# Splitting the output weights of a hybrid attention layer one piece at a time instead of back to back

## The chip, the cores and the metric

The kernel is one program on one core of a Trainium2 chip. The number that counts is the device time of one execution in microseconds; lower is better. Engines: PE (TensorE, matmuls; PEld its weight loads), DVE (VectorE), ACT (ScalarE), POOL (GpSimd), SP (SyncE, which here only issues DMAs). Each engine works through its own list of instructions strictly in order and waits at an instruction until what it needs is there.

## The reference, cut to what matters

Two layers (DEPTH = 2). Each normalises 1280 tokens (256 prompt, 1024 sample), projects them once, runs two mixers on the result, and maps both outputs by one matrix `w_out` back to the model width of 1024. The mixers are multi-head latent attention with 8 heads and a gated DeltaNet with 4 heads.

```python
o_a = mla_attention(q_nope, q_pe, kv[..., :NOPE], kpe_all, kv[..., NOPE:]) * jax.nn.silu(g_a)
...
o_b = rmsnorm(o_b, o_norm).reshape(B, S, D_B) * jax.nn.silu(g_b)
out = jnp.einsum('bse,ed->bsd', jnp.concatenate([o_a, o_b], axis=-1), w_out)
x = x + gate * out
```

Large products are made of three reduced-precision matmuls each: an operand is split into a high part (the value rounded to the fp32r format) and a low part (the value minus the high part), and high·high, high·low and low·high are added. `w_out` (1024 x 1024) is one of the operands that are split, once per layer.

## The kernel before

**Stages of a layer.** Input projection (tiles `zp`, weights `wh`/`wl`), DeltaNet scans, then attention head by head, then the output stage (`wop`). Attention runs beside the end of the DeltaNet work. It is done in the transposed form: keys on the partitions, 512 queries in each of two halves along the free axis.

**One attention head, `main(h)`.** For the sample tokens it walks 10 key tiles of 128 keys (kt = 2 to 11). Per key tile PE makes the scores of each half in three matmuls (`sp`), ACT makes their exponentials (`pe<-sp`, 128x512 each), and PE multiplies the exponentials of the tile before with the values (`po`). The sum of the exponentials over the keys is kept apart: the tiles `pe` are added into an accumulator (`pe<-pe,pe`, 128x1024) on POOL, except at key tiles 7 and 11 and for the very last tile, where DVE adds (`VADD`, `VLAST`). So a head has six adds on POOL and three on DVE, and the last three links of this chain are a POOL add, a DVE add and the final DVE add. `finish(h)` then sums the accumulator over the partitions with a matmul (`pd`), takes the reciprocal on DVE, multiplies by the gate on POOL and by the output on DVE (`ob`), and writes the result to DRAM. A shorter block for the 256 prompt tokens (128x256 tiles) stands at the start of each head.

**Beside it, `prep(h+1)`.** The keys and queries of the next head are projected (`kp`, `qp`), and for each query the largest score is found (`pm` matmuls, DVE reduces `at<-pm`). These maxima are transposed (`mxt`), written to DRAM (`mx_d<-at`) and read back as one row (`at<-mx_d`), which the next head's scores need.

**The output weights, `pre_c`.** A thread of its own that starts when the last DeltaNet head is done. It loads `w_out` in 16 pieces of 128x512 into a ring of 8 buffers `wor`, and splits each piece with `split_wo`: ACT casts the high part (`woh<-wor`) and POOL subtracts for the low part (`wol<-wor,woh`). A load of piece 9 or later waits until the piece that had its buffer has been split. After the last piece `pre_c` starts the threads of the output stage.

**What sets the order.** All work is written as Python generators ("threads"). `Sched.run` (line 105) keeps a clock per engine with estimated costs and hands out the instruction that can start earliest, ties by a priority table `PR`; `pre_c` has the lowest priority among the attention threads (`prec` = 5). A thread can `yield` the name of a flag and is not continued before some thread has set it. `main` sets a flag `m{h}.{kt-2}` at each key tile of head h (line 1582); `prep` uses these flags to pace itself. The result is one fixed list per engine. When the estimate leaves PE idle for long, the scheduler puts in small filler matmuls (`spare`).

**Names.** Tile names carry running numbers that differ between the two programs; `pe_8841` and `wol_9012` are numbers of layer 0, `pe_19174` of layer 1. All instructions come from one helper, so in the profile they all stand on line L312.

Of the kernel before, what the change touches and what calls it, by code (L numbers as in the profile page):

```python
# [16 lines left out]
P = 128  # L17
# [7 lines left out]
NK = T + PAST  # L25
DEPTH = 2
HA = 8
# [367 lines left out]
def body(tc, I, O):  # L395
# [8 lines left out]
    def open_pool(stack, name, bufs=1, **k):  # L404
        return Pool(stack.enter_context(tc.tile_pool(name=name, bufs=bufs, **k)), bufs)
# [153 lines left out]
    def mixer(l, hhl):  # L559
        sd = Sched()  # L560
# [831 lines left out]
        def open_rest():  # L1392
            nonlocal bp
            ws.close()
            bp = open_pool(bs, f"b{l}", bufs=1, side="right")
            t5 = hp.tile([P, 4096], F32R, tag="hh2", name="at5")
            t6 = hp.tile([P, 4096], F32R, tag="hl2", name="at6")
            f6 = t6[:, NK:].bitcast(F32)
            at["ga"] = [f6[:, 0:640], f6[:, 640:1280]]
            at["ob"] = [bp.tile([P, 512], F32, tag=f"ob{i}", name=f"ob{i}") for i in range(2)]  # L1400
            wv = at["wv"] = bp.tile([P, 512], F32, tag="wv", name="wv")
            SY.dma_start(wv, I["w_v"][l])
            Kt.append((t5[:, 0:NK], t6[:, 0:NK]))
            Q.append((t5[:, NK : NK + T], t5[:, NK + T : NK + 2 * T]))
            for h in range(HA):
                if h:
                    sd.add(PR['prep'], prep(h))
                if h % 2 == 0:
                    sd.add(PR['vv'], vproj(h // 2))
                sd.add(PR['main'], main(h))  # L1410
            sd.add(PR['prec'], pre_c())
# [228 lines left out]
        def pre_c():  # L1640
            yield f"done{HB-1}"
            gs.close()
            cw = open_pool(cs, f"cw{l}", bufs=1)
            xs_ = ExitStack()
            cx = open_pool(xs_, f"cx{l}", bufs=1)
            yield 0
            for e in range(8):
                hi = cw.tile([P, DM], F32R, tag=f"woh{e}", name=f"woh{e}")
                lo = cw.tile([P, DM], F32R, tag=f"wol{e}", name=f"wol{e}")
                wo.append((hi, lo))  # L1650
                for hf in range(2):
                    raw = cx.tile([P, 512], F32, tag="wor", name="wor", bufs=8)
                    sl = slice(hf * 512, hf * 512 + 512)
                    SY.dma_start(raw, I["w_out"][l, e * P : (e + 1) * P, sl])
                    wor.append((hi[:, sl], lo[:, sl], raw))
                    yield 0
                    if len(wor) >= 8:
                        split_wo(wor.pop(0), e)
            while wor:
                split_wo(wor.pop(0), len(wor) // 2)  # L1660
                yield 0
            xs_.close()
            c0 = open_pool(cs, f"c0{l}", bufs=1)
            cc_[0] = c0
            load_gate(0, c0)
            for t in range(2):
                sq[t] = c0.tile([P, 2], F32, tag=f"sq{t}", name="sq")
            sd.add(PR['ldc'], load_c())
            sd.add(PR['mm'], mm_thread())

        wor = []

        def split_wo(w, e):
            hi, lo, raw = w
            S.copy(hi, raw)
            (V if len(wor) % 2 < VWO else G).tensor_tensor(lo, raw, hi.bitcast(F32), op=ALU.subtract)
# [14 lines left out]
        def load_c():  # L1691
            for t in range(NT):
                if t == 1:
                    yield f"main{HA-2}"
                    yield f"vv{HA//2-1}"
                    yield f"prep{HA-1}"
                    m1 = hp.tile([P, 4, DM], F32, tag="hh1", name="m1")
                    n1 = hp.tile([P, 2, 8, P], F32R, tag="hl1", name="n1")
                    x, of, cc_["tm"] = m1[:, 0], m1[:, 1].rearrange("p (a b) -> p a b", a=8), m1[:, 2]
                elif t == 2:  # L1700
                    yield "tm0"
                    yield "C"
                if t >= 3:
                    yield f"fin{t-3}"
                if t != 1:
                    x = cc_[0 if t % 3 == 0 else 1].tile([P, DM], F32, tag="x", name="x", bufs=1 if t % 3 == 0 else 2)
                SY.dma_start(x, (I["x"] if l == 0 else xs)[t * P : (t + 1) * P, :])
                if t == 0:
                    yield "attn0"
                pool = cc_.get(t % 2)  # L1710
                if t != 1:
                    of = pool.tile([P, 8, P], F32, tag="of", name="of")
                SY.dma_start(of, o_d[:, :, t * P : (t + 1) * P].rearrange("e p t -> p e t"))
                if t >= 2:
                    yield f"mm{t-2}"
                if t == 1:
                    oh, ol = n1[:, 0], n1[:, 1]
                else:
                    oh = pool.tile([P, 8, P], F32R, tag="oh", name="oh")
                    ol = pool.tile([P, 8, P], F32R, tag="ol", name="ol")  # L1720
                V.tensor_copy(oh, of)
                G.tensor_tensor(ol, of, oh.bitcast(F32), op=ALU.subtract)
                yield 0
                xt[t], ot[t] = x, (oh, ol)
                sd.flag(f"ld{t}")

        def load_gate(t, pool):
            gb[t] = pool.tile([P, DM], F32, tag="gbc", name="gbc", bufs=1)
            SY.dma_start(gb[t], gate_d[l, t // 2 : t // 2 + 1, :].to_broadcast([P, DM]))
# [25 lines left out]
        def mm_thread():  # L1755
            for t in range(NT):
                yield f"ld{t}"
                oh, ol = ot[t]
                x = xt[t]
                if t < 2:  # L1760
                    s2[t], jk = sq[t], cc_[0].tile([P, 512], mybir.dt.bfloat16, tag="jk", name="jk")
                else:
                    s2[t], jk = [cc_[1].tile([P, n], d, tag=f"s{n}", name=f"s{n}", bufs=3 if n == 2 else 1) for n, d in ((2, F32), (512, mybir.dt.bfloat16))]
                for hf in range(2):
                    pt = yield from bank("wop")
                    cs = slice(hf * 512, hf * 512 + 512)
                    for e in range(8):
                        for i, (a, w) in enumerate(((oh, wo[e][0]), (oh, wo[e][1]), (ol, wo[e][0]))):
                            PE.matmul(pt, a[:, e, :], w[:, cs], start=(e == 0 and i == 0), stop=(e == 7 and i == 2))
                        yield 0  # L1770
                    if t == 1:
                        tm = cc_["tm"][:, cs]
                    elif t:
                        tm = cc_[1].tile([P, 512], F32, tag="tm", name="tm", bufs=2)
                    else:
                        tm = cc_[0].tile([P, 512], F32, tag="of", name="tm0")
                    with sd.side(1):
                        V.tensor_tensor(tm, pt, gb[0 if t < 2 else 2][:, cs], op=ALU.mult)
                        free(pt)
                        V.tensor_tensor(x[:, cs], x[:, cs], tm, op=ALU.add)  # L1780
                        S.activation(jk, x[:, cs], AF.Square, accum_out=s2[t][:, hf : hf + 1])
                        if hf:
                            sd.add(PR['fc'], fin(t))
                    if not t and hf:
                        sd.flag("tm0")
                sd.flag(f"mm{t}")
# [43 lines left out]
    for l in range(DEPTH):  # L1830
        hhl = mixer(l, hhl)
# [78 lines left out]
```

## Time and profile before

| | us |
|---|---|
| median of 3 runs | 2221.69 |
| lowest, highest | 2219.49, 2224.27 |
| the profiled execution | 2217.9 |
| its span in the trace | 2216.1 |
| PE busy | 2097.0 (95%) |
| DVE busy | 1442.9 (65%) |
| POOL busy | 847.4 (38%) |
| ACT busy | 771.0 (35%) |
| mean granted clock of PE | 0.986 |

The trace is one execution taken by the hardware profiler; its times run from the span's start. An idle stretch is put down to what ended it. The clock that PE was granted is given as a share of 2.4 GHz; it has two levels, 1.0 (2.4 GHz) and 0.5 (1.2 GHz). Attention of layer 0 lies at about 690 to 1042 us, that of layer 1 at about 1730 to 2099 us; the output weights are split at 826 to 880 us and 1884 to 1931 us, during heads 2 and 3 of each layer.

### The profile page before, as it was taken

To read this page: it belongs to the slowest core of one execution; us is meant where nothing else is said; L and a number is where in the kernel's file an instruction comes from. 1 tells how busy PE (TensorE), PEld (TensorE's weight loads), DVE (VectorE), ACT (ScalarE), POOL (GpSimd) and SP (SyncE) were. 2 spreads that over 40 slices of the span, in tenths; PEclk is the share of its full clock that TensorE was granted. 3 is DMA by queue.
4 is the path that set the end of the run, shared out by engine and by line. 5 is a ranking of instruction groups with operands and counts; after the bars stand their busy time and mean duration, and the time that the engine had idled before them with its cause. 6 is when DMAs were issued, how large, how long until landed. Compare 5 with 4: busy or idle time off the path is not lost. (4 is left out here: it accounts for less than half of the span.)

```text
span 2216.1 us, 35036 instructions
## 1 busy us (share of the span) xinstructions
PE 2097.0 (95%) x12154; PEld 1519.9 (69%) x12154; DVE 1442.9 (65%) x3085; ACT 771.0 (35%) x2120; POOL 847.4 (38%) x757
## 2 busy tenths in 40 slices
PE   8899999989989998999999999998998999899998
PEld 6676778778666654555777777887876665455576
DVE  4767476686585765564667783887749576665454
ACT  4244224242124344443222441433222434544311
POOL 2343222352415247445331442144341524735521
PEclk9999999989999999999999999999999999999999
DMA  7376776856764322101423654677875441310153
GB/s 276 118 240 196 250 223 194 237 168 209 221 168 150 101 83 71 34 18 50 148 101 95 196 163 151 191 219 216 255 248 158 116 136 53 100 33 19 41 161 110
DMA packets 388481, 327.88 MB, mean 148 GB/s; under 512 B 88736, under 2 KB 326784, under 8 KB 388048
## 3 DMA queue, kind: packets, MB, share of 16 engines
q1 hardware_dynamic: 388304, 325.63, 48.9%
q8 instruction: 97, 1.59, 0.3%
q14 instruction: 80, 0.66, 0.1%
HBM read 220.08 MB, written 105.46 MB: 147 GB/s over the span
## 5 line engine op out<-in xcount | busy, mean ns | idle before, releaser
L312 PE MATMUL zp<-hh,wh 128*128 128x512 f32 (+2 forms) x1128 | 421.5, 374 | 8.4 <-DVE ai L312 6.9
L312 PE MATMUL zp<-hh,wl 128*128 128x512 f32 (+2 forms) x1128 | 421.1, 373 | 4.1 <-POOL wl L312 3.8
L312 PE MATMUL zp<-hl,wh 128*128 128x512 f32 (+2 forms) x1128 | 420.6, 373 | 3.2 <-POOL hl L312 3.1
L312 POOL TENSOR_TENSOR wl<-wr,wh 128x512 fp32r<-128x512 f32 (+1 forms) x114 | 156.2, 1370 | 400.8 <-DVE wh L312 231.5
L312 ACT ACTIVATE pe<-sp 128x512 f32<-128x512 f32 (+1 forms) x352 | 201.6, 578 | 259.0 <-PE sp L312 243.5
L312 DVE TENSOR_REDUCE at<-pm 128x1 f32<-128x512 f32 (+1 forms) x336 | 212.3, 683 | 80.2 <-PE pm L312 79.3
L312 POOL TENSOR_TENSOR pe<-pe,pe 128x1024 f32<-128x1024 f32 x96 | 229.3, 2388 | 80.8 <-DVE pe L312 51.4
L312 PEld LDWEIGHTS zp<-hh,wh 128*128 128x128 f32 (+1 forms) x1128 | 214.1, 190 | 41.9 <-DVE ai L312 7.1
L312 PE MATMUL sp<-at 97*128 97x512 f32 (+1 forms) x704 | 239.9, 408 | 2.6 <-ACT pe L312 1.5
L312 PEld LDWEIGHTS zp<-hh,wl 128*128 128x128 f32 (+1 forms) x1128 | 214.0, 190 | 38.0 <-issue 5.6
L312 PEld LDWEIGHTS zp<-hl,wh 128*128 128x128 f32 (+1 forms) x1128 | 214.2, 190 | 36.3 <-POOL hl L312 4.5
L312 PE MATMUL po<-pe,vv 128*64 128x512 f32 (+1 forms) x768 | 187.1, 563 | 3.4 <-ACT pe L312 2.6
L312 PEld LDWEIGHTS sp<-at 97*128 97x128 f32 x704 | 123.3, 189 | 88.5 <-issue 56.1
L312 POOL TENSOR_SCALAR kpt<-ktok,kdb 128x128 f32<-128x128 f32 x160 | 130.0, 824 | 94.1 <-DMA ai_d<-kpt 84.4
L312 PE MATMUL pm<-at 96*128 96x512 f32 (+1 forms) x416 | 129.2, 385 | 7.9 <-ACT at L312 4.6
L312 PE MATMUL sp<-at,at 97*128 97x512 f32 (+1 forms) x352 | 136.5, 388 | 0.0
L312 DVE TENSOR_TENSOR pe<-pe,pe 128x256 f32<-128x256 f32 (+1 forms) x64 | 79.5, 1244 | 83.9 <-POOL pe L312 43.4
L312 PE MATMUL wop<-woh,ol 128*128 128x512 f32 x288 | 114.4, 397 | 2.2 <-POOL ol L312 2.2
L312 PE MATMUL wop<-woh,oh 128*128 128x512 f32 x288 | 114.5, 398 | 0.0
L312 PE MATMUL wop<-wol,oh 128*128 128x512 f32 x288 | 114.3, 397 | 0.0
L312 PEld LDWEIGHTS pm<-at 96*128 96x128 f32 x416 | 70.9, 191 | 61.5 <-ACT pe L312 21.4
L312 DVE TENSOR_TENSOR wtmp<-blk,W 104x31 f32<-104x31 f32 (+15 forms) x248 | 105.6, 426 | 4.6 <-POOL W L312 0.9
(267 smaller groups left out, 3860.7 us busy)
## 6 DMA issues: line engine op xcount, KB each, us to landing
wr<-in_w_main SPq DMA_DIRECT2D x116, 256.0 KB
ti<-ai_d SPq DMA_DIRECT2D x144, 192.0 KB
ai_d<-ai SPq DMA_DIRECT2D x80, 256.0 KB
kc<-kqv_d SPq DMA_DIRECT2D x160, 128.0 KB
wa<-in_w_ada SPq DMA_DIRECT2D x64, 256.0 KB
kqv_d<-yc SPq DMA_DIRECT2D x48, 256.5 KB
kq<-kqv_d SPq DMA_DIRECT2D x16, 641.0 KB
rb<-grow_d SPq DMA_DIRECT2D x80, 128.0 KB
```

The costliest lines, as they stand in the source:

```text
L312: op = Op(lambda: f(*a, **k), self.key, self.ns(name, a, k, aps), outs, [x for x in aps if x is not acc])
```

## The change

`pre_c` no longer splits a piece as soon as the scheduler finds room. Before each split it yields a flag of attention progress: a list holds the flags of every other key tile of heads 0 to 6 (five per head); the first time, the flags already set are counted, and from there each piece takes the next flag. When the list is used up, a piece waits for nothing.

```diff
                     wor.append((hi[:, sl], lo[:, sl], raw))
                     yield 0
                     if len(wor) >= 8:
+                        yield from turn()
                         split_wo(wor.pop(0), e)
             while wor:
+                yield from turn()
                 split_wo(wor.pop(0), len(wor) // 2)
                 yield 0
...
-        wor = []
+        wor, slots = [], []
+
+        def turn():
+
+            todo = [f"m{h}.{i}" for h in range(HA - 1) for i in range(0, NK // P - 2, 2)]
+            if not slots:
+                slots.append(sum(x in sd.flags for x in todo))
+            i = slots[0]
+            slots[0] += 1
+            yield todo[i] if i < len(todo) else 0
```

What this does to the engines' lists is seen best on POOL at the end of head 2 in layer 0. There `pe_8841` is the accumulator of head 2, the next `pe_` number that of head 3, `wol` the low part of a piece, `ob` the output of a head and `at` the queries of the head after. Before:

```order
L312 TENSOR_TENSOR pe_8841<-pe_8841,pe 128x1024 x3
L312 TENSOR_TENSOR wol_9012<-wor,woh_9011 128x512
L312 TENSOR_TENSOR pe_8841<-pe_8841,pe 128x1024
L312 TENSOR_TENSOR wol_9012<-wor,woh_9011 128x512
L312 TENSOR_TENSOR pe_8841<-pe_8841,pe 128x1024
L312 TENSOR_TENSOR wol_9020<-wor,woh_9019 128x512
L312 TENSOR_TENSOR pe_8841<-pe_8841,pe 128x1024
L312 TENSOR_TENSOR wol_9020<-wor,woh_9019 128x512
L312 TENSOR_TENSOR wol_9035<-wor,woh_9034 128x512 x2
L312 TENSOR_TENSOR wol_9051<-wor,woh_9050 128x512 x2
L312 TENSOR_TENSOR ob_7082<-at_7080,ob_7082 128x512
```

Here eight pieces stand in head 2, five of them between the head's last POOL add and its `ob`.

The same place after the change, from the same first add on:

```order
L312 TENSOR_TENSOR pe_8841<-pe_8841,pe 128x1024 x5
L312 TENSOR_TENSOR wol_9012<-wor,woh_9011 128x512
L312 TENSOR_TENSOR pe_8841<-pe_8841,pe 128x1024
L312 TENSOR_TENSOR ob_7082<-at_7080,ob_7082 128x512
L312 TENSOR_TENSOR wol_9012<-wor,woh_9011 128x512
L312 TENSOR_TENSOR at_6486<-at_6488,at_6486 96x256
L312 TENSOR_TENSOR wol_9020<-wor,woh_9019 128x512
L312 TENSOR_TENSOR ob_7081<-at_7080,ob_7081 128x128
L312 TENSOR_TENSOR pe_9188<-pe_9188,pe 128x1024
L312 TENSOR_TENSOR at_6486<-at_6488,at_6486 96x512 x2
L312 TENSOR_TENSOR pe_9188<-pe_9188,pe 128x1024
L312 TENSOR_TENSOR wol_9020<-wor,woh_9019 128x512
```

One piece is left in head 2, ahead of its last POOL add, and nothing stands between that add and `ob`. The other fifteen pieces go to heads 3, 4 and 5, five each; in each of these heads one piece stands ahead of the last POOL add and one at the place of the DVE add of key tile 7. Layer 1 has the same pattern.

On SP the loads of the later pieces move too. The maxima of head 4 go out as `mx_d_4`; the loads of the second half of the ring are the `wor` rows. Before, in layer 0, behind the fetch of head 3's gates:

```order
L312 DMA wor<-in_w_out 128x512 x5
L312 DMA o_d<-ob_7082 64x512 x2
L312 DMA o_d<-ob_7081 64x128 x2
L312 DMA gbc<-gate_d 128x1024
L312 DMA x<-in_x 128x1024
L312 DMA mx_d_4_9485<-at_6488 10x128
```

The remaining loads stand in one row, and the outputs of a whole head lie between them and `mx_d_4`.

After the change, the same stretch:

```order
L312 DMA wor<-in_w_out 128x512
L312 DMA o_d<-ob_7082 64x512 x2
L312 DMA wor<-in_w_out 128x512
L312 DMA o_d<-ob_7081 64x128 x2
L312 DMA wor<-in_w_out 128x512 x3
L312 DMA mx_d_4_9420<-at_6488 10x128
L312 DMA at_6486<-mx_d_4_9420 1x1280
```

Three loads, each of which waits for a split on POOL, now stand directly ahead of `mx_d_4`; of the two last loads none stands ahead of a later head's maxima without a head's output between.

## Rows read from the trace of the kernel before

**Rows 1.** The page: busy us (share of the span) xinstructions of each engine.
```profile
PE 2097.0 (95%) x12154; PEld 1519.9 (69%) x12154; DVE 1442.9 (65%) x3085; ACT 771.0 (35%) x2120; POOL 847.4 (38%) x757
```
**Rows 2.** Waits of PE, whole span: who for whom, us in total, times, longest.
```profile
PE pd L312 <- DVE pe L312: 11.0, 3, 5.5
```
**Rows 3.** Busy time by stretch, layer 0, from reciprocal to reciprocal: heads 2, 3, 4; sum of heads 2 to 7.
```profile
798.51:846.35 47.84, 40.87 (x184) 21.43 (x182) 30.46 (x39) 20.69 (x39) 27.92 (x18) 0.95 0.40 127
846.35:885.75 39.40, 38.41 (x158) 19.81 (x159) 24.79 (x33) 21.25 (x40) 31.10 (x20) 0.97 0.14 42
885.75:927.80 42.05, 41.80 (x196) 22.74 (x197) 24.86 (x35) 19.28 (x36) 19.23 (x11) 1.00 0.12 30
...
sum 243.07, PE 234.16 PEld 124.04 DVE 139.63 ACT 110.96 POOL 137.83; mean PE 39.03 PEld 20.67 DVE 23.27 ACT 18.49 POOL 22.97
```
**Rows 4.** The same for layer 1: heads 2 and 3, and the sum.
```profile
1854.27:1899.99 45.72, 39.31 (x170) 20.30 (x166) 28.51 (x37) 18.57 (x34) 25.50 (x16) 0.96 0.40 122
1899.99:1945.69 45.70, 44.52 (x188) 23.28 (x189) 28.74 (x35) 24.09 (x46) 32.97 (x22) 0.93 0.20 61
...
sum 244.80, PE 235.50 PEld 124.92 DVE 141.94 ACT 110.36 POOL 137.12; mean PE 39.25 PEld 20.82 DVE 23.66 ACT 18.39 POOL 22.85
```
**Rows 5.** Timeline, layer 0, end of head 2: start, us, engine, operation [idle before <-releaser].
```profile
836.90 4.96 POOL L312 TENSOR_TENSOR wol<-wor,woh 128x512 fp32r<-128x512 f32 x4
836.98 5.96 DVE L312 TENSOR_TENSOR pe<-pe,pe 128x1024 f32<-128x1024 f32 x1 [6.92 <-POOL pe L312]
844.32 1.98 PE L312 MATMUL pd<-pe,twos 128*64 128x512 f32 x4 [5.47 <-DVE pe L312]
```
**Rows 6.** Timeline, layer 1, end of head 2.
```profile
1891.80 3.71 POOL L312 TENSOR_TENSOR wol<-wor,woh 128x512 fp32r<-128x512 f32 x3
1891.88 6.04 DVE L312 TENSOR_TENSOR pe<-pe,pe 128x1024 f32<-128x1024 f32 x2 [6.70 <-ACT woh L312]
1897.97 1.97 PE L312 MATMUL pd<-pe,twos 128*64 128x512 f32 x4 [5.26 <-DVE pe L312]
```
**Rows 7.** Busy time by stretch, just behind these two waits (PEclk third from last).
```profile
844.32:848.67 4.35, 4.35 (x13) 1.31 (x13) 2.61 (x2) 0.00 (x0) 0.00 (x0) 0.53 0.00 2
...
1897.97:1906.50 8.53, 8.53 (x29) 3.55 (x29) 5.84 (x4) 2.73 (x6) 2.98 (x3) 0.50 0.14 45
```
**Rows 8.** Timeline, layer 1, head 3: three pieces at the DVE add of key tile 7.
```profile
1927.20 3.78 POOL L312 TENSOR_TENSOR wol<-wor,woh 128x512 fp32r<-128x512 f32 x3
1927.60 4.46 DVE L312 TENSOR_TENSOR pe<-pe,pe 128x1024 f32<-128x1024 f32 x1
1932.72 0.50 PE L312 MATMUL pm<-at 96*128 96x512 f32 x1 [1.18 <-DVE at L312]
```
**Rows 9.** Timeline, layer 0, end of head 4, no piece near: the final add and its matmul.
```profile
925.12 1.23 DVE L312 TENSOR_TENSOR pe<-pe,pe 128x1024 f32<-128x1024 f32 x1 [1.39 <-ACT pe L312]
926.67 1.08 PE L312 MATMUL pd<-pe,twos 128*64 128x512 f32 x4
```
**Rows 10.** Timeline, layer 0, end of head 3: a piece ahead of the last POOL add.
```profile
878.36 1.28 POOL L312 TENSOR_TENSOR wol<-wor,woh 128x512 fp32r<-128x512 f32 x1
883.34 1.23 DVE L312 TENSOR_TENSOR pe<-pe,pe 128x1024 f32<-128x1024 f32 x1
884.62 1.08 PE L312 MATMUL pd<-pe,twos 128*64 128x512 f32 x4
```
**Rows 11.** The pieces' own instructions: duration ns min/median/max, first and last start.
```profile
L312 ACT CAST woh<-wor x32: 607/611/630, 825.5 to 1927.1; 128x512 fp32r<-128x512 f32 x32
L312 POOL TENSOR_TENSOR wol<-wor,woh x32: 1263/1277/1308, 826.2 to 1929.7; 128x512 fp32r<-128x512 f32 x32
```
**Rows 12.** Timeline, layer 0: maxima on SP at two head ends, and the scores that need them.
```profile
831.67 0.30 SPq L312 DMA_DIRECT2D mx_d<-at  x1
...
924.92 0.23 SPq L312 DMA_DIRECT2D at<-mx_d  x1
927.68 0.50 PE L312 MATMUL sp<-at 97*128 97x256 f32 x2
```

## The prediction

> **What bounds the kernel now.** I read the engine shares first, then PE's waits, then busy time cut by attention head, then the timeline where a head stood out. The shares say that PE is the bound: 2097.0 of 2216.1 us are busy, and POOL and ACT, which carry the split, are under 40% [rows 1]. Moving the split can therefore pay only where PE waits because of it. PE's waits name one such place: `pd` waits for the accumulator (`pe`) on DVE, three times, 11.0 us together [rows 2].
>
> Cutting the trace by head shows where. In layer 0 head 2 takes 47.84 us, and PE is busy for 40.87 of them; head 4, in which nothing is split, takes 42.05 and has PE busy for 41.80 [rows 3]. In layer 1 it is head 2 again, 39.31 of 45.72 [rows 4]. Over heads 2 to 7 PE is idle for 243.07 - 234.16 = 8.9 us in layer 0 and 244.80 - 235.50 = 9.3 us in layer 1.
>
> The timeline of the two head ends gives the mechanism. POOL runs four pieces back to back from 836.90 to 841.86; the DVE add that starts at 836.98 lasts 5.96 us; `pd` waits 5.47 us for it and for the final add behind it [rows 5]. An add of this size takes 1.23 us where POOL is quiet [rows 9]. In layer 1 three pieces run from 1891.80 to 1895.51, the two DVE adds take 6.04 us instead of 2 x 1.23, and the first of them was also late, at 1891.88 after 6.70 us of idle; `pd` waits 5.26 us [rows 6]. In both, the stretched add ends about one undisturbed add after the run of pieces does: a DVE add whose operands both lie in SBUF hardly gets on while POOL runs such pieces without a pause.
>
> The idle has a second price. Behind it PE runs with a granted clock share of 0.53 for 4.35 us in layer 0 and 0.50, which is the lower level of 1.2 GHz, for 8.53 us in layer 1 [rows 7]. In head 4 of layer 0, with 0.25 us idle, it is 1.00 throughout [rows 3].
>
> **The change part by part.** *Instructions.* Nothing is added or removed: 32 casts of 0.611 us on ACT and 32 subtractions of 1.277 us on POOL stay [rows 11]. All of them move, with the 32 loads on SP.
>
> *What goes.* (a) The waits at the two head ends: 5.47 + 5.26 = 10.73 us [rows 5, 6]. After the change no piece stands between the last POOL add of a head and its `ob`, so no piece can run beside the last two DVE adds. (b) The slow clock behind them: 4.35 x (1 - 0.53) + 8.53 x (1 - 0.50) = 2.04 + 4.27 = 6.31 us [rows 7]. (c) In head 3 of layer 1 three pieces meet the DVE add of key tile 7, which takes 4.46 us, and `pm` waits 1.18 us behind it [rows 8]. One piece stands there in future. Together 10.73 + 6.31 + 1.18 = 18.2 us.
>
> *What comes, at head ends.* Four heads of each layer (2 to 5) now have one piece ahead of the last POOL add, so the chain POOL add, DVE add, final add starts up to 1.28 us later, eight times. Upper bound 8 x 1.28 = 10.2 us. The trace has this arrangement once: at the end of head 3 of layer 0 a piece runs at 878.36, the final add ends at 884.57, and `pd` starts at 884.62 with no wait on record [rows 10]; at an end without a piece the add ends at 926.35 and `pd` starts at 926.67, none either [rows 9]. The last exponentials are what the final add waits for, the piece lies beside them. Lower bound therefore 0, and below nothing by no more than fractions of the 0.25 us idle of a quiet head. I take 0.2 us each, nearer to the row that shows it: 1.6 us.
>
> *What comes, at key tile 7.* In three heads of each layer one piece can meet a DVE add, and behind that add on DVE stand the reduces that free the `pm` banks. Rows 8 give the slack: the add was 4.46 - 1.23 = 3.23 us late and PE lost 1.18, so 2.05 us are free. One piece delays the add by at most 1.28, under that. I take 0; upper bound 6 x 1.18 = 7.1 us, were the slack elsewhere nil.
>
> *What comes, in between.* A piece puts 0.611 us on ACT ahead of exponentials that PE waits for. Head 3 of layer 0, into which nine of its sixteen pieces reach, has 39.40 - 38.41 = 0.99 us of idle against 0.25 in head 4 [rows 3], so at most 0.08 us per piece. The number of pieces stays, so I take 0; if all of it came anew, 32 x 0.08 = 2.6 us.
>
> *The loads.* Behind each `wor` row on SP now stands something later: outputs `ob`, which have two buffers and time, and twice per layer (ends of heads 2 and 3) the maxima of the next head. Its scores run 2.76 us after the read-back is issued (924.92 to 927.68) [rows 12]. The piece those loads wait for is the one ahead of the last POOL add but one or at it, and by the order of PE the transpose of the maxima comes after it, so I take 0. What it would cost is the third rival.
>
> *Sum.* 18.2 - 1.6 = 16.6 us: 2217.9 - 16.6 = 2201.3 on the profiled execution. That execution was 3.8 us faster than the median of the runs, 2221.69; from the median it is 2205.1. What will be compared is a median, but the terms are from the faster one; I say 2204.
>
> *A rule held against this.* The rows show that the DVE add in layer 0 was held through four POOL instructions, 5.96 us [rows 5]. The Trainium skill, "SBUF — State Buffer", section "SBUF: two separate sides", has DVE instructions with two SBUF inputs and GpSimd instructions contend for one port pair by an exclusive lock, held "for the whole instruction". By that rule an add waits for one POOL instruction, not for a run of them. Then a lone piece does to an add what a run does, and spreading saves nothing there. The rows contradict the first half: 5.96 us is more than one piece of 1.28 and an add of 1.23 together. The second half is the first rival below, told from rows.
>
> **The rivals.** *First: half of it comes back.* Each lone piece still meets a DVE add or holds a chain back by its own length. Price: 8 x 1.28 = 10.2 us at the head ends, leaving a gain of 8 us, or 2210 to 2214. For it: an add in front of `pd` was visibly stretched both times that pieces stood near [rows 5, 6], and in the new order `pd` of head 2 stands right behind `po`, with the short block of the next head no longer ahead of it as cover. Against it: rows 10.
>
> *Second: no change.* The pieces cost what they cost, and PE waits in eight smaller portions: 8 x 1.28 plus 6 x 1.18 plus 2.6 = 19.9 us against 18.2, so 2218 to 2223. It needs every upper bound at once, and at waits near 1.2 us also no lower clock.
>
> *Third: slower, through SP.* SP is in order. The three `wor` loads ahead of `mx_d_4`, and the ninth ahead of `mx_d_3`, wait for POOL; if POOL runs late there, the maxima go out late and the next head's scores stand still, at two head ends in each layer. It decides when the maxima go out later by more than the slack of the read-back; I bound that slack by the 1.0 us between `pd` at 926.67 and these scores at 927.68 [rows 9, 12]. Price, if it is as bad as the waits of today: 4 x (5.3 + 3.1) = 33.6 us with the clock, so 2217.9 - 18.2 + 33.6 = 2233. For it: in layer 0 `mx_d` went out at 831.67, amid the first pieces [rows 12]. Against it: POOL is busy for 19.23 of 42.05 us in a quiet head [rows 3], and five pieces of 1.28 make that 25.6, so it need not fall behind by more than a piece.
>
> **How the numbers follow.** The forecast, a gain of 13 to 20 us (2199 to 2208), has 0.66; the first rival 0.20 (2209 to 2216); no change 0.08; slower 0.06. About 0.2%, 4.4 us, is what a measurement of this kernel can tell from no change: faster means under 2217.2. Forecast and first rival make faster 0.86, the second makes same 0.08, the third slower 0.06. The range holds forecast and first rival but for its last bit: 2198 to 2215.
>
> **What would show it.** Right: `pd` no longer among PE's longest waits; heads 2 and 3 together near 80 us in both layers (87.2 and 91.4 today [rows 3, 4]); granted clock 1.00 in heads 2 and 3; no DVE add above 2.6 us in attention; PE idle near 4 us per layer over heads 2 to 7. First rival: `pd` waits of about 1 us at heads 2 to 5. Third: scores waiting for `at` by DMA at the start of heads 3 and 4. Wrong altogether, if heads 2 and 3 keep their length with no piece beside its last adds: then the pieces were not what held `pd`.

## The result, and the profile after

The changed kernel takes 2196.87 us (median of 4 runs, 2190.64 to 2203.65), the kernel before beside it 2220.94 (2219.49 to 2224.27): a ratio of 0.989, 95% interval 0.9859 to 0.9922. The gain is 24.1 us; forecast were 16.6 and a time of 2204 (2198 to 2215). The interval is that of a gain of 17 to 31 us. The direction came, the forecast gain was too small, and the measured time lies 1.1 us under the range.

The profiled execution took 2190.64 us, its span 2188.9. The engine shares of its page, which answer to [rows 1]:

```profile
PE 2084.9 (95%) x12150; PEld 1516.2 (69%) x12150; DVE 1433.2 (65%) x3085; ACT 769.1 (35%) x2120; POOL 849.9 (39%) x757
```

PE is busy 12 us less. Busy time by head after the change, layer 0, heads 2 to 4 and the sum of heads 2 to 7, to be read against [rows 3]:

```profile
796.62:836.53 39.91, 38.53 (x172) 20.46 (x171) 25.49 (x37) 16.82 (x31) 20.62 (x12) 1.00 0.37 109
836.53:877.03 40.50, 40.45 (x195) 23.38 (x197) 24.92 (x34) 21.40 (x41) 25.95 (x16) 1.00 0.21 60
877.03:916.00 38.97, 38.41 (x172) 20.42 (x169) 24.94 (x34) 19.77 (x38) 25.39 (x16) 1.00 0.11 30
...
sum 232.73, PE 230.50 PEld 124.40 DVE 135.27 ACT 109.73 POOL 137.58; mean PE 38.42 PEld 20.73 DVE 22.55 ACT 18.29 POOL 22.93
```

The sum of layer 1, against [rows 4]:

```profile
sum 232.08, PE 230.08 PEld 123.92 DVE 134.85 ACT 109.54 POOL 137.56; mean PE 38.35 PEld 20.65 DVE 22.47 ACT 18.26 POOL 22.93
```

Heads 2 to 7 are 10.34 us shorter in layer 0 and 12.72 in layer 1, together 23.06: nearly the whole gain of the medians lies there. PE's idle time in them fell from 18.2 us to 4.2, and the granted clock is 1.00 in every head. This stage repeats well: in two experiments that leave layer 0 as it is after the change (dose_sub, dose_sub2), its sum is 232.73 and 232.76. So the sums of these heads, read from one profile of each kernel, are the measure below; the four runs of the changed kernel scatter by 13 us.

The end of head 2 in layer 0 after the change (POOL, DVE and PE rows of the timeline), against [rows 5]:

```profile
828.44 1.28 POOL L312 TENSOR_TENSOR wol<-wor,woh 128x512 fp32r<-128x512 f32 x1 [0.67 <-DMA wor<-in_w_out]
829.67 2.38 POOL L312 TENSOR_TENSOR pe<-pe,pe 128x1024 f32<-128x1024 f32 x1
832.09 1.23 DVE L312 TENSOR_TENSOR pe<-pe,pe 128x1024 f32<-128x1024 f32 x1 [3.92 <-POOL pe L312]
833.86 1.23 DVE L312 TENSOR_TENSOR pe<-pe,pe 128x1024 f32<-128x1024 f32 x1 [0.54 <-ACT pe L312]
835.41 1.08 PE L312 MATMUL pd<-pe,twos 128*64 128x512 f32 x4
```

One piece stands ahead of the last POOL add, none beside the DVE adds; both take 1.23 us, the final one waits for exponentials and not for POOL, and `pd` has no wait. PE's longest waits in heads 2 to 7 of layer 0 no longer name `pd` [rows 2]:

```profile
PE po L312 <- ACT pe L312: 1.1, 2, 0.6
PE sp L312 <- ACT at L312: 0.5, 1, 0.5
```

And all adds of exponentials on DVE (ns: shortest, median, longest); the longest was 5956 before:

```profile
L312 DVE TENSOR_TENSOR pe<-pe,pe x64: 360/1224/1708, 684.2 to 2066.6; 128x1024 f32<-128x1024 f32 x48, 128x256 f32<-128x256 f32 x16
```

### The profile page after: what moved, and what is told of

Read it like the earlier page. It is cut to its first block, busy times and chain, and to the rows that moved or that the text cites. A ratio compares the mean times of both kernels' runs of the same rounds, so it can differ in the third digit from the quotient of the medians.

```text
span 2188.9 us, 35021 instructions
## 1 busy us (share of the span) xinstructions
PE 2084.9 (95%) x12150; PEld 1516.2 (69%) x12150; DVE 1433.2 (65%) x3085; ACT 769.1 (35%) x2120; POOL 849.9 (39%) x757
## 5 line engine op out<-in xcount | busy, mean ns | idle before, releaser
L312 DVE TENSOR_TENSOR pe<-pe,pe 128x256 f32<-128x256 f32 (+1 forms) x64 | 68.7, 1073 | 68.8 <-POOL pe L312 44.0
```

The source lines that it names most:

```text
L312: op = Op(lambda: f(*a, **k), self.key, self.ns(name, a, k, aps), outs, [x for x in aps if x is not acc])
```

## The experiments

The question was where the 23.06 us came from, 6.5 more than the sum. A *piece* is POOL's subtraction for 128x512 of the weights. An add is *held* when it lasts longer than its 1.23 us because POOL works beside it. The theories: **hold** (in the first expectations called run theory): POOL's run of pieces holds DVE's last adds, `pd` waits, and a slow clock follows; **lateness** (or bulk): pieces standing ahead of POOL's own adds make the chain late, held or not; **spreading**: pieces cost wherever they lie close together; **order**: moving the pieces lets the scheduler place other instructions and fillers (`spare`) differently, and that is the gain.

| kernel | heads 2 to 7, layer 0 | layer 1 | whole kernel |
|---|---|---|---|
| before | 243.07 | 244.80 | 2220.94 |
| after | 232.73 | 232.08 | 2196.87 (0.9859 to 0.9922) |
| set_pieces | 234.99 | 234.21 | 2205.87, one run |
| gap | 246.27 | 242.88 | 0.999 (0.9972 to 1.0009) |
| noend | 243.94 | 241.42 | 0.9999 (0.998 to 1.0018) |
| noend_nofill | 243.09 | 241.32 | 2216.87, one run |
| burst_end | 243.66 | 245.33 | 2228.85, one run |
| burst_mid | 237.97 | 237.26 | 2211.91, one run |
| odd | 235.39 | 235.53 | 2206.78, one run |
| no_last | 233.77 | 233.12 | 0.9915 (0.9882 to 0.9947) |
| after_nofill | 232.01 | 231.53 | 0.9893 (0.987 to 0.9916) |

Ratios are to the kernel before on the same chip; the sums are in us, as is a time without a ratio.

**Hold without moving anything: set_pieces.**

```diff
+    class Set:
+        def tensor_tensor(self, out, *a, **k):
+            nc.gpsimd.memset(out.bitcast(F32), 0.0)
+            nc.gpsimd.memset(scr_[0], 0.0)
+
+    GG, scr_ = Eng(Set(), "G"), [None]
...
+            scr_[0] = f6[:, 1280:2048]
...
-            (V if len(wor) % 2 < VWO else G).tensor_tensor(lo, raw, hi.bitcast(F32), op=ALU.subtract)
+            GG.tensor_tensor(lo, raw, hi.bitcast(F32), op=ALU.subtract)
```

The second memset writes 128x768 of scratch; the low part of the weights is left at zero.

> The kernel before, instruction for instruction in the same order, but POOL's part of a piece is two memsets of about the same length together (one of them on the low part, which leaves the low part of the output weights at zero) in place of the subtraction; memsets did not hold DVE in dose_set. This keeps POOL as late as before and takes away only the hold on DVE. Hold theory: no DVE add above 1.5 us; pd waits fall by the stretch of its adds, from 5.47 to about 0.7 and from 5.26 to about 1.8; the wait of pm (1.18) is gone; granted clock 1.00; heads 2 to 7 at 235 to 237 us in place of 243.1 and 244.8. Lateness theory (pieces standing ahead of POOL's adds make the chain late, held or not): both pd waits stay above 4 us, sums above 241.

The end of head 2, layer 0: first the last POOL add in the kernel before, then POOL, DVE and PE of set_pieces, all its adds on DVE, and the sums of both layers:

```profile
834.58 2.37 POOL L312 TENSOR_TENSOR pe<-pe,pe 128x1024 f32<-128x1024 f32 x1
```
```profile
834.03 2.38 POOL L312 TENSOR_TENSOR pe<-pe,pe 128x1024 f32<-128x1024 f32 x1
836.36 0.52 POOL L412 MEMSET wol<- 128x512 f32 x1
836.45 1.23 DVE L312 TENSOR_TENSOR pe<-pe,pe 128x1024 f32<-128x1024 f32 x1 [4.10 <-POOL pe L312]
...
838.03 1.22 DVE L312 TENSOR_TENSOR pe<-pe,pe 128x1024 f32<-128x1024 f32 x1 [0.36 <-ACT pe L312]
...
840.95 1.03 PE L312 MATMUL pd<-pe,twos 128*64 128x512 f32 x4
```
```profile
L312 DVE TENSOR_TENSOR pe<-pe,pe x64: 360/1216/2055, 688.4 to 2080.5; 128x1024 f32<-128x1024 f32 x48, 128x256 f32<-128x256 f32 x16
```
```profile
sum 234.99, PE 231.67 PEld 123.73 DVE 134.75 ACT 111.03 POOL 136.50; mean PE 38.61 PEld 20.62 DVE 22.46 ACT 18.51 POOL 22.75
```
```profile
sum 234.21, PE 230.99 PEld 123.69 DVE 134.37 ACT 110.37 POOL 135.34; mean PE 38.50 PEld 20.61 DVE 22.39 ACT 18.39 POOL 22.56
```

POOL is as late as before but for 0.54 us (its last add ended at 836.95 then, at 836.41 here) and memsets fill the time in which the four pieces ran, but the adds take 1.23 and 1.22 us and `pd` has no wait. The clock stays at 1.00 in these heads. Only one add is still stretched, to 2.06, beside a subtraction of queries. The two sums fall by 8.08 and 10.59, together 18.67 us, a little more than I forecast (235 to 237 us). The one run of the whole kernel, 2205.87 us, is 8 us under the fastest of nine runs of the kernel before on that chip. So hold and what follows it is 18.7 of the 23.1 us, and lateness alone is not enough to make `pd` wait. What is left between this kernel and the changed one, 2.26 + 2.13 = 4.4 us, I call order: pieces that hold nothing, in the old places against the new ones. It is a remainder, traced only in part (below).

**Gaps in the run: gap.**

```diff
+    class Gap:
+        def tensor_tensor(self, out, *a, **k):
+            nc.gpsimd.tensor_tensor(out, *a, **k)
+            nc.gpsimd.tensor_copy(scr_[0], out[:, 511:512])
```

The piece's subtraction goes through this class, as in set_pieces.

> The kernel before, with its order on PE, DVE, ACT and SP and its order of pieces, but behind each piece POOL copies one column of the piece's result to a scratch column, so that the next piece cannot start right behind it. Run theory (what hurts is that POOL's next piece follows without a gap, so that the DVE add gets in only behind the whole run): no DVE add above 2.6 us, pd waits of at most 2.5 us each in place of 5.5 and 5.3, granted clock 1.00, heads 2 to 7 at 235 to 239 us per layer (243.1 and 244.8 before). Order theory (the loss lay in where pd, fillers and loads stand): unchanged, 243 to 246 us. Bulk theory (POOL's work near a head's end delays DVE whatever its spacing): pd waits of 5 us or more stay.

The end of head 2, layer 0:

```profile
838.58 1.27 POOL L412 TENSOR_TENSOR wol<-wor,woh 128x512 fp32r<-128x512 f32 x1
838.65 4.95 DVE L312 TENSOR_TENSOR pe<-pe,pe 128x1024 f32<-128x1024 f32 x3 [7.76 <-POOL pe L312]
839.91 1.06 POOL L413 CAST at<-wol 128x1 fp32r<-128x1 f32 x1
840.93 1.26 POOL L412 TENSOR_TENSOR wol<-wor,woh 128x512 fp32r<-128x512 f32 x1
...
843.33 1.12 PE L312 MATMUL pd<-pe,twos 128*64 128x512 f32 x2 [3.64 <-DVE pe L312]
```

The adds beside pieces are held one piece at a time (2.27 and 2.24 us of the 4.95, at most 2.30 anywhere); one add of 3.54 us stands beside two subtractions of queries, between which no copy stands. But the copies also delay POOL: its last add ends 1.67 us later than before, and `pd` still waits 3.64 and 3.83 us, with 1.2 GHz behind both; in layer 0 `pm` waits 2.13 us behind the add of 3.54, again with 1.2 GHz behind it, and so that sum came out above the one of before. My numbers for the sums failed. The run shows that a gap lets DVE in, and that hold and lateness add up in one chain; it can't price either.

**A dose of held adds: dose_sub, dose_sub2, dose_set.** In layer 1 of the changed kernel:

```diff
                                 (V if kt in VADD else G).tensor_tensor(acc[:, :, :n], acc[:, :, :n], prev[1][:, :, :n], op=ALU.add)
+                                if l and 3 <= h <= 6 and kt == 10:
+                                    for i in range(h - 2):
+                                        G.tensor_tensor(at["scr"][i % 2], at["wv"], at["wv"], op=ALU.subtract)
```

This is dose_sub2; dose_sub writes one destination, dose_set has a memset of 128x1280 in place of the subtraction.

> The changed kernel with 1, 2, 3 and 4 extra POOL subtractions of 128x512 behind the last POOL add of heads 3, 4, 5 and 6 of layer 1 only; their results are used by nothing. Run theory: the DVE add beside them takes 1.2 + 1.3 n us up to the end of the run, about 2.4, 3.7, 5.0, 6.2; pd waits 0 to 0.5, 1 to 2, 2.5 to 3.5 and 4 to 5; behind the last two also slow clock. By the rule of one lock per instruction the add takes at most 2.5 us whatever n, and pd waits at most 1.3 at each end. Order theory: no pd wait at all; the order on PE and DVE is that of the changed kernel.

> The changed kernel with 1, 2, 3 and 4 extra POOL subtractions of 128x512 behind the last POOL add of heads 3 to 6 of layer 1, as in dose_sub, but with two destinations in turn, so that they can follow one another without the 0.08 us gap. Run theory with the lock kept over a gapless run: the DVE add beside them is held to 1.1 us behind the end of the run wherever the first piece starts before it (up to 6 us), pd waits up to 4 us in heads 5 and 6, layer 1's sum 236 to 242 us in place of 232.1. If the lock is handed over at any boundary: adds of at most 2.6 us, sum 232 to 233 us as in dose_sub.

> The same places, but 1, 2, 3 and 4 POOL memsets of 128x1280 (about 1.2 us each, reading nothing) in place of the subtractions. If it is the common read port that DVE lacks: DVE adds stay at 1.2 to 1.3 us and pd does not wait; layer 1's heads 2 to 7 stay at 232 us. If any POOL instruction holds DVE, the rows are those of the subtractions. If POOL's own in-order list did it (ob late), both dose runs would show the same loss with undisturbed adds.

Sums of layer 1: 232.30, 232.08 and 232.15 us; `pd` waits for an add in none. With one destination (dose_sub) POOL's subtractions follow each other with gaps of 0.08 us and the adds took at most 2.05 us, so the doses that I forecast never came. With two, one add was kept behind two more pieces, in head 5:

```profile
2004.33 3.05 POOL L312 TENSOR_TENSOR at<-wv 128x512 fp32r<-128x512 f32 x3
...
2005.13 4.66 DVE L312 TENSOR_TENSOR pe<-pe,pe 128x1024 f32<-128x1024 f32 x2
...
2010.89 0.65 PE L312 MATMUL pd<-pe,twos 128*64 128x512 f32 x2
```

The first of these two adds took 3.33 us, 2.1 more than alone, and `pd` 1.1 us behind the second did not wait: at that head end of the changed order a hold of 2.1 us is covered. Beside four memsets (dose_set) both adds took 1.23.

**No pieces at head ends: noend, noend_nofill.**

```diff
-            todo = [f"m{h}.{i}" for h in range(HA - 1) for i in range(0, NK // P - 2, 2)]
...
-            yield todo[i] if i < len(todo) else 0
+            on = [(h, i) for h in range(HA) for i in range(NK // P - 2) if f"m{h}.{i}" in sd.flags]
+            h, i = on[-1]
+            yield f"m{h + 1}.0" if i >= 6 and h < HA - 1 else 0
```

Here `on[-1]` is the last flag that is set. noend_nofill also keeps the scheduler from placing fillers from the end of the scans to the end of attention.

> Sum of heads 2 to 7 was 243.1 and 244.8 us before, 232.7 and 232.1 after. Run theory (the loss was only the run of pieces on POOL beside a head's last DVE adds): pieces packed as closely as before, but none at head ends, give back nearly all, 232 to 236 us in each layer, and no wait of pd; whole kernel within 6 us of the changed one. Spreading theory (the pieces cost wherever they lie close together): heads 3 and 4, which hold eight each, stay long, 238 us or more per layer, a gain of at most half of the 24 us.

> The kernel with no pieces at head ends (noend), whose heads 2 to 7 took 243.9 and 241.4 us with 58 filler matmuls in each layer, about 6.6 us of PE time, now without any filler from the end of the scans to the end of attention; every other instruction stands in the same place. If the fillers ate its gain: 236 to 239 us in each layer and granted clock still 1.00. If they only stood where PE would have waited anyway: 242 to 245 us with 6 us more PE idle, and perhaps a lower clock.

This was my worst forecast. In noend no `pd` wait on a DVE add is left, no clock is lost in these heads, no add is above 2.3 us, and the whole kernel gains nothing; the two sums together are only 2.5 us shorter than before. Its fillers in heads 2 to 7 of layer 0 (count, busy us, mean ns):

```profile
L433 PE MATMUL spare<-ident 128*128 128x128 f32 x58 | 8.0, 282 | 0.0
```

After the change there are 6. Without them (noend_nofill) the sums fell by only 0.85 and 0.10: the fillers mostly stood where PE had to wait. In both layers `pd` then waits 3.00 us, and the clock falls behind it, but what it waits for is DVE's reduces (`at`) for the next head, and scores wait 1.19 and 1.13 us for the read-back of the maxima. With sixteen pieces packed into heads 3 and 4, most of what the clear ends gave is lost again. In size this is what I forecast for spreading. No piece stands beside the waits named here (in layer 0 the last one ahead of the wait of 3.00 ends at 860.9 us, the wait begins at 876.9), so I put the loss down to order; this run alone can't separate the two. The simple form of my theory, keep the ends clear and all is won, is refuted.

**Bursts: burst_end, burst_mid.** `todo = [f"m{h}.8" for h in range(2, HA - 2) for _ in range(4)]`, and `m{h}.1` for heads 3 to 6, each list taken from its start.

> Four pieces at the end of each of heads 2 to 5, two or three of them behind the last POOL add. Run theory: a DVE add of 3.5 to 5 us and a pd wait of 2 to 4 us at each of the eight ends, with slow clock behind some; PE idle over heads 2 to 7 of 12 to 18 us per layer, the sum 244 to 255 us in each layer. Order theory (what helped were the other places of fillers, loads and pd in the engines' lists, not POOL): no row of pd waits, sum 232 to 238 us.

> Four pieces at the second key tile of each of heads 3 to 6, no piece near a head's end. Hold theory: no DVE add at a head end is stretched and pd does not wait; 232 to 235 us per layer unless the scheduler adds fillers. Spreading theory (pieces cost wherever they lie close together, through ACT's casts ahead of the exponentials): 238 us or more per layer, with PE waiting for exponentials behind each burst.

burst_end, head 4 of both layers, the same place in the program: the run of pieces, the two adds, `pd`:

```profile
920.68 3.50 POOL L312 TENSOR_TENSOR wol<-wor,woh 128x512 fp32r<-128x512 f32 x2
920.77 4.48 DVE L312 TENSOR_TENSOR pe<-pe,pe 128x1024 f32<-128x1024 f32 x2 [5.19 <-POOL pe L312]
...
925.32 1.08 PE L312 MATMUL pd<-pe,twos 128*64 128x512 f32 x4 [1.72 <-DVE pe L312]
```
```profile
1982.53 2.52 POOL L312 TENSOR_TENSOR wol<-wor,woh 128x512 fp32r<-128x512 f32 x2
1982.63 4.83 DVE L312 TENSOR_TENSOR pe<-pe,pe 128x1024 f32<-128x1024 f32 x2 [5.18 <-POOL pe L312]
...
1987.51 1.80 PE L312 MATMUL pd<-pe,twos 128*64 128x512 f32 x4 [2.06 <-DVE pe L312]
```

In the first DVE gets in behind one piece, and POOL's second piece is held instead; in the second DVE is kept behind both. Of all its adds only this one was kept behind two pieces. `pd` waits 6.8 us together, four times at the eight ends for 1.3 to 2.1 us, and PE is idle for 8.3 and 8.9 us per layer: both less than forecast. The sums of 243.7 and 245.3 lie at the edge of my range (244 to 255), and partly for another reason:

```profile
PE pd L312 <- DVE pe L312: 6.8, 5, 2.1
PE kp L312 <- DMA at<-in_w_hd: 4.9, 2, 2.7
```

SP's wait in layer 1, and the load that stood behind it:

```profile
SPq L312 <- POOL wol L312: 5.1, 1, 5.1
```
```profile
2030.13 0.34 SPq L312 DMA_DIRECT2D gbc<-gate_d  x1
```

`kp` waits for the weights of the next head. SP stood 5.1 us at the load of the output stage's gate (`gbc`), which `pre_c` issues behind the last piece and which waited here for POOL's `wol`; the weights were issued behind it, at 2031.01. In layer 0 it was 5.2 us. That is the prediction's third rival as a mechanism, at another transfer than the ones I named; it did not happen in the change. burst_mid has no held add at a head's end, stays above my 232 to 235 us, and loses 5.2 us per layer to the changed kernel: it has 24 fillers per layer in place of 6, and waits of `pm` of 1.03 (for ACT) and 1.20 us (for DVE) in each. The first of these waits stands ahead of the bursts, the second behind an add that a subtraction of queries stretched to 2.30 us, and behind head 2 its one wait for exponentials is the 0.56 us that the changed kernel has too. So as far as its waits show, close packing costs here through order, and not through the exponentials as the spreading theory has it.

**Other slots: odd, no_last, after_nofill.** `range(1, NK // P - 2, 2)`; `range(0, NK // P - 4, 2)`; no fillers during attention.

> The change with the other key tiles (second, fourth and so on): one piece now stands right behind the last POOL add of heads 2 to 5, beside the DVE add of the head's end. Hold theory with a cover of about 2 us at a head end: adds of 2.3 us there, no pd wait above 0.5, sums 232 to 234 us as in the changed kernel. First rival of the prediction (a lone piece costs its own length): pd waits of about 1 us in four heads of each layer, sums 236 to 238.

> The change with four turns per head, without that of the last key tile but one, so that no piece stands ahead of a head's last POOL add; the pieces reach one head further. If a piece there costs nothing, as the changed kernel's trace says: 232 to 233.5 us in each layer, the whole kernel within 3 us of the changed one. If it costs 0.2 us each: 0.8 us less per layer.

> The changed kernel without the 6 filler matmuls that each layer has in heads 2 to 7 (1.05 us of PE time net) and those of head 1; everything else in the same place. If fillers cost their own time: 231.7 and 231.0 us in place of 232.7 and 232.1, the whole kernel 1 to 3 us faster than the changed one, too little to tell by the clock of whole runs. If PE waits there anyway: the same sums, 232.7 and 232.1.

In odd a lone piece stands beside the adds at head ends; they take 1.86 to 2.22 us and `pd` does not wait, so a lone piece does not cost its own length. The sums are nevertheless 2.7 and 3.5 us longer than after the change; two waits of `pm` for ACT of 1.03 us in each layer are part of that. no_last has the changed kernel's ends without the piece ahead of the last POOL add and gains nothing by it (1.0 us longer in each layer); it has 14 fillers per layer. after_nofill is 0.7 and 0.55 us shorter in these heads, as far as its fillers go; its ratio is that of the change. No version is shown to beat the changed kernel.

## Why the prediction was wrong in size, point by point

*What bounds, and the mechanism of the loss:* right. PE's waits at two head ends, held DVE adds, slow clock behind them: set_pieces removes these alone and gains 18.67 us; the sum had 10.73 + 6.31 + 1.18 = 18.2. The clock term was read rightly: by the granted clock the low stretches of before cost an estimated 2.05 and 4.30 us, and in these heads after the change there are none. As a general statement, that an add "hardly gets on" while POOL runs pieces without a pause is too strong (last section).

*The signs.* `pd`, the clock, the longest add (1.71 us) and heads 2 and 3 (80.41 and 79.77 us, forecast near 80) came as said. PE's idle did not: 2.2 and 2.0 us per layer, where I had said near 4.

*The step that failed* is what comes in return: "I take 0.2 us each", a cost of 1.6 us at head ends, and 0 for everything else that the new order moves. In its place the new order gave 4.4 us (set_pieces to after): 2.3 of idle and 2.1 of PE's busy time. Of the idle, set_pieces has waits of 0.82, 0.45, 1.03 and 0.56 us which the changed kernel does not have, and the changed kernel has two of 0.56 of its own, net 1.74. The 0.45, 1.03 and 0.56 lie in heads in which set_pieces has no piece; the 0.82 lies in head 3 of layer 0 behind ACT, where pieces still run, and may be theirs. In the busy part, fillers fell from 10 to 6 in layer 1; in layer 0 they stayed at 6, and its 1.2 us of busy time I can't name. 4.4 + 1.6 makes 6.0 of the 6.5 us, and the other 0.5 is the gone part, 18.7 for 18.2. Nothing in the prediction bounded what a new order can give below zero: its bound was "fractions of the 0.25 us idle of a quiet head". Heads 5 and 6 of layer 1 before, without a piece as well, would have told me more:

```profile
1985.32:2026.93 41.61, 40.58 (x195) 23.04 (x197) 24.58 (x35) 19.21 (x36) 19.15 (x11) 1.00 0.09 23
2026.93:2066.01 39.08, 38.52 (x172) 20.08 (x169) 24.74 (x35) 17.61 (x33) 19.18 (x11) 1.00 0.07 18
```

Here PE is idle for 1.03 and 0.56 us with no piece in the head, so a quiet head has such waits by its order alone, and another order can lose or win them. The experiments say how large that term is: odd, no_last, burst_mid and the change, none of which has a `pd` wait of note, span 232.1 to 238.0 us per layer, fillers included.

*The range.* Its low end, 2198, allowed a gain of 19.9 us from the profiled execution and of 23.7 from the median of before. What the new places do stood in it as a cost alone, up to 19.9 us in the second rival, and nowhere as a gain. That the whole time fell under 2198 is in part the chance of these runs: dose_set, with the changed kernel's sums in both layers (232.75 and 232.15), took 2204.99 us in its one run, and after_nofill, with shorter sums, 2202.61 as a median. The missed size is shown by the sums, not by the 1.1 us.

*Rivals.* The first (each lone piece costs its length) is refuted by the trace after the change and by odd. The second did not occur here; noend ends at its result, no gain, but by other waits than those it added up. The third did not occur, and its mechanism is real in burst_end.

*The rule.* The Trainium skill, "SBUF — State Buffer", section "SBUF: two separate sides", gives the shared port pair to whichever starts first, for the whole instruction, and has a DVE op with two SBUF inputs contend only against a GpSimd op that reads SBUF. The traces agree with the second part: an add that starts 0.07 to 0.09 us behind a piece takes 2.27 to 2.30 us, some 1.05 more than alone, where it has only this one piece to wait for, and beside memsets 1.23. They do not agree with what the prediction drew from the first part, that an add waits for one instruction and not for a run: see below.

## What to carry to other kernels

Read a long instruction beside another engine's run as a possible hold, and test it by an operation of the same length that doesn't contend, in the same place; that separates the hold from the queue. When a change moves work in a list that a scheduler writes, give the new order a term of both signs, sized by what other orders of the same work differ by: here up to 5.9 us per layer, more than the 1.6 us that I argued over.

## What the hardware showed

Where a POOL subtraction follows another without a gap (it starts 0.03 to 0.07 us before the end of the last), a waiting DVE add gets in or doesn't. In the twelve traces without memsets, a 128x1024 add was unfinished at 25 such boundaries: it was kept waiting over 11 of them, seven of these in the kernel before, and served at 14. Where POOL had a gap of 0.06 to 0.08 us (gap, dose_sub) it was served each of nine times. The two stretches of burst_end show both outcomes at one place of the program. What decides it stays open; so does whether every execution of the kernel before holds its adds as the profiled one did, though the medians differ by as much. Where DVE is served, POOL waits its turn: the second piece took 2.27 us in place of 1.28, and a copy of one column 1.06 in place of 0.18.
